# Hymba encoder layer on one core: the weight-sum unit of eight projection pairs is emitted in another quarter

## The chip, the core and the metric

The kernel runs on one core of a Trainium2 chip. The metric is the device time of one execution in microseconds (us), lower is better. The engines are PE (matrix products), DVE (VectorE), ACT (ScalarE), POOL (GpSimd) and SP, whose queue issues most of the transfers (DMAs). Each engine works through its own list of instructions in order; they wait for one another through semaphores.

## The reference

One bidirectional encoder layer over 1024 prompt rows and 256 sample rows of width 2048:

```python
hn = rmsnorm(x, norm_w)
proj = jnp.einsum('btd,dp->btp', hn, w_in)
na_q, na_k, na_v, na_g, ml_qk, ml_v, ml_o, ml_z, ml_gp = jnp.split(proj, cuts, axis=-1)
att = neighbourhood_attention(na_q, na_k, na_v, na_rpb) * silu(na_g)
qk = silu(centred_depthwise_conv(ml_qk, conv_w, conv_b))
h = rmsnorm(bidirectional_mlstm(mq, mk, mv, gates), head_norm_w)
mem = h * sigmoid(ml_o) * silu(ml_z)
y = x + concat(att, mem) @ w_out
```

After it stands a last rmsnorm of y. Everything is float32.

## The kernel before

Every product is made in three passes: each operand is split into a high part, cast by ACT to the matmul's format (fp32r), and a low part, the difference, made by DVE; PE then forms high*high, high*low and low*high (`split_a`, lines 159 to 161, and `mm_c`).

The stage that the change touches is the input projection of the first 768 rows, `pair_a` (line 328). One call computes a *pair*: two blocks of 128 output columns. It uses a 2x2 block scheme with seven products in place of eight, numbered 1 to 7 and run in the order 1, 5, 6, 4, 7, 2, 3. The sum over the input dimension is cut into four *quarters*, r = 0 to 3. In each quarter

- SP loads 128x1024 raw weights into a buffer of the ring `ra`, which has three (line 367, tile `A48r` for pair A48),
- POOL forms the four weight sums of products 5, 6, 7 and 3 (line 372, tile `A48t`; ring of four),
- ACT casts and DVE subtracts for each of the seven products (lines 160 and 161, tile `A48s`; ring of eight),
- PE runs six matmuls for each product, 42 in a quarter and 168 in a pair (line 190, accumulators `A48b`).

In the last quarter `fold` adds the seven accumulators into the two result tiles `A48c` on DVE (line 340), each read freeing a PSUM bank, and `out_scaled` multiplies by the row scales (line 167). Products 1, 5 and 6 use three banks of one tag, so product 6 of a pair can't start before product 5 of the pair ahead has been folded.

What is left of a pair is done by the generator `finish_a`, stepped while the next pair runs. The order of pairs repeats in fours (`order`): a qk pair, whose convolution (lines 270 to 282) is DVE work during the pair behind it; a v pair (n1 from 56 on, such as A68); and two more. A v pair's result is transposed by PE (line 310, tile `A68v`, 12 small instructions), copied by ACT and stored by SP (line 313), all in the pair that follows it.

Into this stage are put 32 *weight-sum units* (`wsum_unit`, line 316), which work ahead for the output projection at the end of the kernel. A unit loads 128x1024 weights into a buffer of the same ring `ra` with a DMA that POOL issues (line 319), adds and subtracts in four POOL instructions of 128x256 (lines 321 to 324), and stores the result to DRAM (line 326). The units are handed to `pair_a` by the loop over the pairs, by position i. Most pairs take one unit, emitted ahead of the load of quarter r = 1; pairs with i % 4 == 1 take two from i = 6 on, at r = 1 and r = 3; v pairs (i % 4 == 3) take none. The build's scheduler then fixes each engine's order from the emitted program, so a unit's instructions can land among those of the pair ahead.

The pairs right behind a v pair, i % 4 == 0, are A8, A12, A16, A20, A40, A44, A48 and A52.

Of the kernel before, what the change touches and what calls it, by code (L numbers as in the profile page):

```python
# [24 lines left out]
NCH = 56  # L25
# [13 lines left out]
def kernel(  # L39
# [27 lines left out]
    def bank(tag, name):  # L67
        return ps.tile([P, 512], F32, tag=tag, name=name, bufs=3 if tag == "pr" else 5)
# [43 lines left out]
    def x_square(g, i):  # L112
        t, q = divmod(i, 2)
        r0 = GOF[g] + t * P
        raw = wa.tile([P, 1024], F32, tag="ra", name=f"xq{g}_{i}", bufs=NRA)
        DM.dma_start(raw, xtok[r0 : r0 + P, q * 1024 : (q + 1) * 1024])
        S.activation(raw, raw, AF.Square, accum_out=ssq[g][:, t, q : q + 1])

    def x_rstd(g):
        n = GSZ[g] // P  # L120
        rc = rcs[g][:, :n]
        V.tensor_reduce(rc, ssq[g][:, :n], axis=mybir.AxisListType.X, op=ALU.add)
        rsqrt_mean(rc, rc, n, float(D))
# [35 lines left out]
    def split_a(hi, lo, src):  # L159
        S.copy(hi, src)  # L160
        V.tensor_tensor(lo, src, f(hi), op=ALU.subtract)

    def out_scaled(o, src, rb, n):
        if n < KT0:
            V.scalar_tensor_tensor(o, src, float(P) ** -0.5, rb, op0=ALU.mult, op1=ALU.mult)
        else:
            V.tensor_tensor(o, src, rb, op=ALU.mult)  # L167
# [14 lines left out]
    def xop(i, kk, b_):  # L182
        if i == 1:
            return xb11[kk][:, b_]
        g_, c = XSLOT[i]
        return xg[g_, kk][:, b_, c]

    def mm_c(o, w, x, first, last):
        for m, (a_, b_) in enumerate(((0, 0), (0, 1), (1, 0))):
            PE.matmul(o, w(a_), x(b_), start=first and m == 0, stop=last and m == 2)  # L190

    def pc(name):
        return wa.tile([P, GA], F32, tag="pc", name=name, bufs=NPC)

    def wsa(name):
        return wa.tile([P, 2, 256], F32R, tag="wsa", name=name, bufs=NWS)
# [89 lines left out]
    def finish_a(n1, Cn):  # L286
        nm = f"A{n1}"
        for j in range(2):
            if n1 >= NCH:
                break  # L290
            if QK0 <= n1 < OT0:
                ct = n1 - QK0 + j
                DM.dma_start(qb[ct], Cn[j][:, GA - 4 :])
                cv = pc(f"{nm}cv{j}")
                yield from conv_taps(cv, Cn[j], ct, GA - 2, 2)
                DM.dma_start(cD[ct][:, : GA - 2], cv[:, : GA - 2])
            else:
                if OT0 <= n1 < ZT0:
                    S.activation(Cn[j], Cn[j], AF.Tanh, scale=0.5)
                elif n1 >= GT0:  # L300
                    th = pc(f"{nm}th{j}")
                    S.activation(th, Cn[j], AF.Tanh, scale=0.5)
                    V.scalar_tensor_tensor(Cn[j], th, 1.0, Cn[j], op0=ALU.add, op1=ALU.mult)
                DM.dma_start(pT[n1 + j][:, 0:GA], Cn[j])
            yield
        if n1 >= NCH:
            for tt in range(GA // P):
                b = bank("a", f"{nm}v{tt}")
                for j in range(2):
                    PE.transpose(b[:, j * P : (j + 1) * P], Cn[j][:, tt * P : (tt + 1) * P], ident)  # L310
                o = wa.tile([P, 256], F32, tag="vo", name=f"{nm}vo{tt}", bufs=2)
                S.copy(o, b[:, :256])
                DM.dma_start(vD[(n1 - NCH) // 2][tt * P : (tt + 1) * P, :], o)
                yield

    def wsum_unit(u):
        raw = wa.tile([P, 1024], F32, tag="ra", name=f"wsum{u}", bufs=NRA)
        t = raw.rearrange("p (s c) -> p s c", s=4)
        G.dma_start(raw, w_os[u])  # L319
        a11, a12, a21, a22 = (t[:, i] for i in range(4))  # L320
        G.tensor_tensor(a22, a21, a22, op=ALU.add)
        G.tensor_tensor(a21, a11, a21, op=ALU.subtract)
        G.tensor_tensor(a11, a22, a11, op=ALU.subtract)
        G.tensor_tensor(a12, a12, a11, op=ALU.subtract)
        cp, c0 = u // 16, u % 16 * 256
        G.dma_start(sD[cp][:, :, c0 : c0 + 256], t)

    def pair_a(n1, bg=iter(()), hook=None, units=()):
        nm = f"A{n1}"
        tags = ("pr", "pr", "pr", "a", "a", "a", "a")  # L330
        order = (1, 5, 6, 4, 7, 2, 3)
        bk = {i: bank(t, f"{nm}b{i}")[:, :HALF] for i, t in zip(order, tags)}
        Cn = [pc(f"{nm}c{j}") for j in range(2)]
        C = [Cn[q // 2][:, (q % 2) * HALF : (q % 2 + 1) * HALF] for q in range(4)]

        def scaled(q):
            out_scaled(C[q], C[q], rbs[0][:, (q % 2) * HALF : (q % 2 + 1) * HALF], n1)

        def plus(q, src, i):
            V.tensor_tensor(C[q], C[src], bk[i], op=ALU.add)  # L340

        def fold(i):
            if i == 1:
                S.copy(C[0], bk[1])
            elif i == 6:
                plus(1, 0, 6)
            elif i == 7:
                plus(2, 1, 7)
                plus(3, 2, 5)
                plus(1, 1, 5)  # L350
                plus(2, 2, 4)
                scaled(3)
                scaled(2)
            elif i == 2:
                plus(0, 0, 2)
                scaled(0)
            elif i == 3:
                plus(1, 1, 3)
                scaled(1)

        for r in range(4):
            if r == 2 and hook is not None:
                hook()
            if r in (1, 3) and r // 2 < len(units):
                wsum_unit(units[r // 2])
            raw = wa.tile([P, 1024], F32, tag="ra", name=f"{nm}r{r}", bufs=NRA)
            DM.dma_start(raw, w_in[n1 // 2, r])
            A = {(j, f_): raw[:, (2 * j + f_) * 256 :][:, :256] for j in range(2) for f_ in range(2)}

            def summed(i, x, y_, op):  # L370
                t = wa.tile([P, 256], F32, tag="wt", name=f"{nm}t{r}{i}", bufs=NWT)
                G.tensor_tensor(t, x, y_, op=op)
                return t

            src = {1: A[0, 0], 4: A[1, 1], 2: A[0, 1]}
            for i in order:
                if i == 5:
                    src[5] = summed(5, A[1, 0], A[1, 1], ALU.add)
                elif i == 6:
                    src[6] = summed(6, src[5], A[0, 0], ALU.subtract)  # L380
                elif i == 7:
                    src[7] = summed(7, A[0, 0], A[1, 0], ALU.subtract)
                elif i == 3:
                    src[3] = summed(3, A[0, 1], src[6], ALU.subtract)
                t = wsa(f"{nm}s{r}{i}")
                split_a(t[:, 0], t[:, 1], src[i])
                for q in range(2):
                    kk = 2 * r + q
                    mm_c(
                        bk[i], lambda a_: t[:, a_, q * P : (q + 1) * P],  # L390
                        lambda b_: xop(i, kk, b_), kk == 0, kk == 7,
                    )
                if r == 3:
                    fold(i)
                elif i in (5, 4, 2):
                    next(bg, None)
        for _ in bg:
            pass
        return finish_a(n1, Cn)
# [48 lines left out]
    order = [4, 6]  # L448
# [11 lines left out]
    bg = iter(())  # L460
    units = list(range(32))
    for i, n1 in enumerate(order):
        n = 0 if n1 >= NCH else 2 if i % 4 == 1 and 5 < i < 30 else 1
        bg = pair_a(n1, bg, second_pools if i == len(order) - 1 else None, units[:n])
        del units[:n]
        if i == 1:
            gates_a()
        k = i - 4
        if 0 <= k < 8:
            x_square(1, k)  # L470
        if k == 8:
            x_rstd(1)
# [1034 lines left out]
```

## Time and profile before

| what | value |
|---|---|
| time, median of 3 runs | 2667.58 us (2665.68 to 2668.62) |
| time of the profiled execution | 2671.81 us |
| span of its trace, first to last instruction | 2670.1 us |
| mean granted PE clock | 0.991 of full |
| busy share DVE / ACT / POOL | 75% / 52% / 31% |

The span is 1.7 us shorter than the profiled execution's own time; that execution is 4.2 us above the median. A row of a timeline gives the start in us, the length of the stretch in us, the engine, the line of the kernel, what is written and read, the count, and in brackets the idle time before it with what ended it. Rows in which several instructions of one kind follow each other are merged.

### The profile page before, as it was taken

To read this page: it belongs to the slowest core of one execution; us is meant where nothing else is said; L and a number is where in the kernel's file an instruction comes from. 1 tells how busy PE (TensorE), PEld (TensorE's weight loads), DVE (VectorE), ACT (ScalarE), POOL (GpSimd) and SP (SyncE) were. 2 spreads that over 40 slices of the span, in tenths; PEclk is the share of its full clock that TensorE was granted. 3 is DMA by queue.
4 is the path that set the end of the run, shared out by engine and by line. 5 is a ranking of instruction groups with operands and counts; after the bars stand their busy time and mean duration, and the time that the engine had idled before them with its cause. 6 is when DMAs were issued, how large, how long until landed. Compare 5 with 4: busy or idle time off the path is not lost.

```text
span 2670.1 us, 43607 instructions
## 1 busy us (share of the span) xinstructions
PE 2602.4 (97%) x14518; PEld 2382.8 (89%) x14518; DVE 1992.5 (75%) x3962; ACT 1389.2 (52%) x3140; POOL 817.3 (31%) x1021
## 2 busy tenths in 40 slices
PE   8999999999999999999999999999999999999997
PEld 8899999999999999998989989989888878877786
DVE  7868778898878788875487587577567675787775
ACT  7534444444444444453566576566566543566654
POOL 0545566656565565500011011010001000125312
PEclk9999999999999999999999999999999999999999
DMA  6524344434343433454556656655555456779875
GB/s 209 177 91 146 119 158 134 143 118 154 104 149 111 135 119 127 137 176 143 172 166 192 197 153 195 187 158 181 177 180 161 155 177 228 223 252 314 284 225 177
DMA packets 245753, 454.20 MB, mean 170 GB/s; under 512 B 30320, under 2 KB 121624, under 8 KB 245528
## 3 DMA queue, kind: packets, MB, share of 16 engines
q1 hardware_dynamic: 232856, 407.38, 48.3%
q0 software_dynamic: 9216, 33.56, 3.9%
q10 hardware_dynamic: 3456, 10.49, 1.0%
q8 instruction: 114, 1.87, 0.3%
q14 instruction: 111, 0.91, 0.1%
HBM read 368.41 MB, written 82.91 MB: 169 GB/s over the span
## 4 chain that ended last, share of the span: by engine, by line
PE 46%; DMA 7%; DVE 3%; ACT 2%; issue 1%; SPq 1%; POOL 0%; ACTq 0%; POOLq 0%; DVEq 0%
PE pc L514 19%; PE pv L596 4%; PE G00p L1286 3%; PE G11p L1286 3%; PE G10p L1286 2%; PE S L1286 2%; PE G01p L1286 1%; PE A54b L190 1%; PE A52b L190 1%; DMA wr<-in_w_in_dram 1%; DMA nap_0vr<-vD 1%; PE nap_0s L638 1%; PE nap_1s L638 1%; DMA wrS<-in_w_o_dram 0%; PE mlp_2in L942 0%
## 5 line engine op out<-in xcount | busy, mean ns | idle before, releaser
L154 DVE TENSOR_TENSOR ws<-wr,ws 128x512 fp32r<-128x512 f32 x224 | 155.1, 697 | 114.8 <-ACT ws L153 113.9
L153 ACT CAST ws<-wr 128x512 fp32r<-128x512 f32 x224 | 137.5, 619 | 157.8 <-PE pc L514 107.8
L1309 POOL TENSOR_TENSOR y<-y,fn 128x512 f32<-128x512 f32 x40 | 62.5, 1578 | 411.0 <-ACT jk L1308 216.1
L104 POOL TENSOR_SCALAR mls_0r<-mls_0r 128x2 f32<-128x2 f32 x4 | 1.1, 278 | 255.9 <-ACT mls_0jk L1110 255.9
L154 DVE TENSOR_TENSOR ws_S<-wrS,ws_S 128x512 fp32r<-128x512 f32 x64 | 54.5, 883 | 13.9 <-ACT ws_S L153 13.9
L154 DVE TENSOR_TENSOR wsv<-wr_v,wsv 128x512 fp32r<-128x512 f32 x64 | 44.4, 697 | 19.1 <-ACT wsv L153 18.6
L153 ACT CAST wsv<-wr_v 128x512 fp32r<-128x512 f32 x64 | 39.2, 616 | 30.8 <-PE pc L514 18.2
L154 DVE TENSOR_TENSOR ws_G10w<-wrG10w,ws_G10w 128x512 fp32r<-128x512 f32 x56 | 44.4, 816 | 13.4 <-ACT ws_G10w L153 13.2
L1286 PE MATMUL S<-ws_S,xsb 128*128 128x512 f32 x192 | 48.2, 406 | 4.0 <-DVE ws_S L154 2.8
L153 ACT CAST ws_G11w<-wrG11w 128x512 fp32r<-128x512 f32 x56 | 34.6, 620 | 33.2 <-PE G11p L1286 17.3
L154 DVE TENSOR_TENSOR ws_G11w<-wrG11w,ws_G11w 128x512 fp32r<-128x512 f32 x56 | 43.0, 793 | 11.1 <-ACT ws_G11w L153 11.1
L154 DVE TENSOR_TENSOR ws_G01w<-wrG01w,ws_G01w 128x512 fp32r<-128x512 f32 x56 | 45.1, 827 | 8.0 <-ACT ws_G01w L153 6.7
L167 DVE TENSOR_TENSOR pco<-pc,rstdb 128x512 f32<-128x512 f32 x48 | 32.9, 687 | 23.3 <-PE pc L514 22.4
L1286 PEld LDWEIGHTS S<-ws_S,xsb 128*128 128x128 f32 x192 | 36.8, 194 | 14.3 <-DVE ws_S L154 4.5
L276 DVE SCALAR_TENSOR_TENSOR pcv<-pco,cw_sb,pcv 128x516 f32<-128x516 f32 x64 | 47.9, 758 | 0.8 <-ACT pcv L270 0.8
L153 ACT CAST ws_S<-wrS 128x512 fp32r<-128x512 f32 x64 | 37.7, 617 | 18.4 <-PE S L1286 10.8
L319 POOL DMA_DIRECT2D wsum<-in_w_os_dram x32 | 18.5, 577 | 92.2 <-DMA xq<-in_xtok_dram 76.9
L153 ACT CAST ws_G10w<-wrG10w 128x512 fp32r<-128x512 f32 x56 | 33.8, 618 | 23.7 <-PE G10p L1286 10.0
L153 ACT CAST ws_G01w<-wrG01w 128x512 fp32r<-128x512 f32 x56 | 34.3, 619 | 22.7 <-PE G01p L1286 12.4
L514 PE MATMUL pc<-x_2h,ws 128*128 128x512 f32 x112 | 44.6, 398 | 0.9 <-ACT ws L153 0.9
L1286 PE MATMUL S<-ws_S,xsv 128*128 128x512 f32 x192 | 45.3, 393 | 0.0
L514 PE MATMUL pc<-x_6h,ws 128*128 128x512 f32 x112 | 44.5, 397 | 0.5 <-ACT ws L153 0.5
(1824 smaller groups left out, 9335.9 us busy)
## 6 DMA issues: line engine op xcount, KB each, us to landing
wr<-in_w_in_dram SPq DMA_DIRECT2D x112, 512.0 KB
wsum<-in_w_os_dram POOLq DMA_DIRECT2D x32, 512.0 KB, 4.1
sD<-wsum POOLq DMA_DIRECT2D x32, 512.0 KB, 3.3
wr_v<-in_w_in_dram SPq DMA_DIRECT2D x32, 512.0 KB
wrS<-in_w_o_dram SPq DMA_DIRECT2D x64, 256.0 KB
xq<-in_xtok_dram SPq DMA_DIRECT2D x20, 512.0 KB
xr<-in_xtok_dram SPq DMA_DIRECT2D x40, 256.0 KB
wrG00w<-sD SPq DMA_DIRECT2D x32, 256.0 KB
```

Of the source, the lines that this page charges most:

```text
L104: E.tensor_scalar(out, ssum, 1.0 / count, EPS, op0=ALU.mult, op1=ALU.add)
L153: S.copy(hi, src)
L154: V.tensor_tensor(lo, src, f(hi), op=ALU.subtract)
L167: V.tensor_tensor(o, src, rb, op=ALU.mult)
L190: PE.matmul(o, w(a_), x(b_), start=first and m == 0, stop=last and m == 2)
L276: V.scalar_tensor_tensor(dst[:, a:n], src[:, a + j - pad : n + j - pad], cw_sb[:, ct, j : j + 1], dst[:, a:n], op0=ALU.mult, op1=ALU.add,)
L319: G.dma_start(raw, w_os[u])
L514: PE.matmul(pb[j], t[:, wi, c : c + P], xs, start=r == 0 and f_ == 0 and q == 0 and wi == 0 and xs is xh, stop=r == 3 and f_ == 1 and q == ...
L596: PE.matmul(outs[tt], xs[:, tt * P : (tt + 1) * P], t[:, wi, q * w : (q + 1) * w], start=first and m == 0 and (gates or tt % 2 == 0), stop ...
L638: PE.matmul(b[:, :nkeys], qs(a_), ks(b_), start=i == 0, stop=i == 2)
L1286: PE.matmul(bk[s_], x_[:, xi, s_ * P : (s_ + 1) * P], t[:, wi, :512], start=first and m == 0, stop=last and m == 2,)
L1309: G.tensor_tensor(yc, yc, fn[nb], op=ALU.mult)
```

## The change

In a pair that follows a v pair the unit is emitted at r = 3 in place of r = 1. `pair_a` now takes a dictionary from quarter to unit; all other pairs keep their units and quarters, and the units keep their order.

```diff
-    def pair_a(n1, bg=iter(()), hook=None, units=()):
+    def pair_a(n1, bg=iter(()), hook=None, units={}):
...
-            if r in (1, 3) and r // 2 < len(units):
-                wsum_unit(units[r // 2])
+            if r in units:
+                wsum_unit(units[r])
...
-        n = 0 if n1 >= NCH else 2 if i % 4 == 1 and 5 < i < 30 else 1
-        bg = pair_a(n1, bg, second_pools if i == len(order) - 1 else None, units[:n])
-        del units[:n]
+        quarters = [(3,), (1, 3) if 5 < i < 30 else (1,), (1,), ()][i % 4]
+        take = {r: units.pop(0) for r in (quarters if i > 1 else (1,))}
+        bg = pair_a(n1, bg, second_pools if i == len(order) - 1 else None, take)
```

On POOL, at the border of v pair A68 and pair A48, the order before was this (`A68t`, `A48t` are the weight sums of line 372; the number behind a name tells one buffer from the next):

```order
 L372 TENSOR_TENSOR A68t_10451<-A68r_10407 128x256
-L319 DMA wsum_10595<-in_w_os_dram 128x1024
 L372 TENSOR_TENSOR A68t_10479<-A68r_10407,A68t_10430 128x256
 L372 TENSOR_TENSOR A48t_10515<-A48r_10504 128x256
-L321 TENSOR_TENSOR wsum_10595<-wsum_10595 128x256
 L372 TENSOR_TENSOR A48t_10532<-A48t_10515,A48r_10504 128x256
-L322 TENSOR_TENSOR wsum_10595<-wsum_10595 128x256
 L372 TENSOR_TENSOR A48t_10558<-A48r_10504 128x256
-L323 TENSOR_TENSOR wsum_10595<-wsum_10595 128x256
 L372 TENSOR_TENSOR A48t_10584<-A48r_10504,A48t_10532 128x256
-L324 TENSOR_TENSOR wsum_10595<-wsum_10595 128x256
```

The unit's load, its four sums and, one row further down, its store leave this place; the pair's own sums of the first quarter now stand there alone.

Further down on POOL, among the sums of A48's second and third quarter, the order of the changed kernel is this:

```order
L372 TENSOR_TENSOR A48t_10649<-A48r_10595 128x256
L319 DMA wsum_10759<-in_w_os_dram 128x1024
L372 TENSOR_TENSOR A48t_10675<-A48r_10595,A48t_10623 128x256
L321 TENSOR_TENSOR wsum_10759<-wsum_10759 128x256
L322 TENSOR_TENSOR wsum_10759<-wsum_10759 128x256
L372 TENSOR_TENSOR A48t_10697<-A48r_10686 128x256
L323 TENSOR_TENSOR wsum_10759<-wsum_10759 128x256
L372 TENSOR_TENSOR A48t_10708<-A48t_10697,A48r_10686 128x256
L324 TENSOR_TENSOR wsum_10759<-wsum_10759 128x256
L372 TENSOR_TENSOR A48t_10728<-A48r_10686 128x256
L326 DMA sD_162<-wsum_10759 512x1x256
```

The load now stands ahead of the last sum of the second quarter, the four sums behind it and among the sums of the third.

On SP the loads of the raw weights move with the ring (`cD` are the stores of the convolved qk pair, `vD` those of the transposed v pair):

```order
 L367 DMA A48r_10504<-in_w_in_dram 128x1024
+L367 DMA A48r_10595<-in_w_in_dram 128x1024
 L296 DMA cD_157<-A36cv_10194 128x766
 L296 DMA cD_158<-A36cv_10317 128x766
-L367 DMA A48r_10602<-in_w_in_dram 128x1024
-L367 DMA A48r_10693<-in_w_in_dram 128x1024
+L367 DMA A48r_10686<-in_w_in_dram 128x1024
 L367 DMA A48r_10766<-in_w_in_dram 128x1024
-L367 DMA A50r_10860<-in_w_in_dram 128x1024
 L313 DMA vD_125<-A68vo_10529 128x256
 L313 DMA vD_125<-A68vo_10555 128x256
 L313 DMA vD_125<-A68vo_10581 128x256
```

The load of A48's second quarter goes ahead of the stores `cD`; the first load of the next pair, A50, goes behind the third store `vD`. DVE's instructions are the same in the same order throughout; those of PE and ACT are too, but for the pairs A8 and A12, where some transposes and one squaring of rows of x (line 117) stand a few places later.

## Prediction

> **What bounds the kernel now.** I read the busy shares first, then the groups of instructions by line for PE, then the timelines of PE, DVE and POOL around one place.
>
> ```profile
> PE 2602.4 (97%) x14518; PEld 2382.8 (89%) x14518; DVE 1992.5 (75%) x3962; ACT 1389.2 (52%) x3140; POOL 817.3 (31%) x1021
> ```
>
> PE is busy nearly all the time, so time is won only where PE waits or runs slowly. The groups show where that is in the stage of the pairs (columns: count, then busy us and mean ns of one, then idle time ahead of them with its releaser).
>
> ```profile
> L190 PE MATMUL A12b<-xg,A12s 128*128 128x384 f32 x144 | 29.6, 360 | 2.9 <-DVE A58c L340 2.9
> L190 PE MATMUL A40b<-xg,A40s 128*128 128x384 f32 x144 | 28.8, 352 | 2.6 <-DVE A64c L340 2.6
> L190 PE MATMUL A48b<-xg,A48s 128*128 128x384 f32 x144 | 28.6, 351 | 3.0 <-DVE A68c L340 3.0
> L190 PE MATMUL A8b<-xg,A8s 128*128 128x384 f32 x144 | 27.3, 340 | 3.0 <-DVE A56c L340 2.9
> ...
> L190 PE MATMUL A56b<-xg,A56s 128*128 128x384 f32 x144 | 25.6, 334 | 0.0
> ```
>
> A pair costs 25.6 us in this group with no idle time (A56). The eight pairs behind a v pair are the exception: each waits 2.6 to 3.1 us for line 340, the fold of the v pair on DVE, and its matmuls are longer by 1.7 (A8) to 4.0 us (A12); the four rows not shown lie at A48's numbers within 0.2 us. These eight are also the pairs whose unit moves. I take A48 as the pattern.
>
> ```profile
> 190.05 1.20 PE L190 MATMUL A56b<-xb,A56s 128*128 128x384 f32 x6
> 219.18 1.20 PE L190 MATMUL A8b<-xb,A8s 128*128 128x384 f32 x6
> 957.27 1.20 PE L190 MATMUL A48b<-xb,A48s 128*128 128x384 f32 x6
> 958.49 1.28 PE L190 MATMUL A48b<-xg,A48s 128*128 128x384 f32 x6
> 962.73 1.30 PE L190 MATMUL A48b<-xg,A48s 128*128 128x384 f32 x6 [2.95 <-DVE A68c L340]
> 965.74 0.42 PE L310 MATMUL A68v<-ident,A68c 128*128 128x128 f32 x1
> 977.76 1.23 PE L190 MATMUL A48b<-xb,A48s 128*128 128x384 f32 x6
> 992.85 1.20 PE L190 MATMUL A50b<-xb,A50s 128*128 128x384 f32 x6
> ```
>
> A pair without loss takes 219.18 - 190.05 = 29.13 us, 0.173 us for each of 168 matmuls. A48 takes 992.85 - 957.27 = 35.58, so it loses 6.45. The parts: product 5 starts 0.18 late (958.49 against 957.27 + 6 x 0.173 = 958.31); product 6 starts 3.20 late (962.73 against 958.49 + 1.04 = 959.53); then the clock.
>
> ```profile
> 223.00:227.00 4.00, 2.33 (x12) 2.04 (x12) 4.00 (x9) 0.41 (x1) 0.91 (x2) 1.00 0.68 227
> 961.00:965.00 4.00, 2.27 (x10) 2.30 (x11) 4.00 (x10) 0.41 (x1) 0.91 (x2) 0.86 0.67 211
> 965.00:969.00 4.00, 4.00 (x19) 3.74 (x19) 4.00 (x8) 0.43 (x2) 1.94 (x3) 0.71 0.27 105
> ```
>
> In these stretches of 4 us (busy time of PE, PEld, DVE, ACT, POOL, then the granted clock) A48's clock falls to 0.86 and 0.71 behind its wait: (0.14 + 0.29) x 4 = 1.72 us lost. A8's stays at 1.00. What is left of A48's loss, 6.45 - 0.18 - 3.20 - 1.72 = 1.35, goes to the 12 transposes of line 310 and their seams. And DVE is busy for the whole 4.00 us of all three: here DVE, not PE, sets the pace.
>
> **What makes DVE late, and what the change removes.** DVE's timeline at that place, then POOL's:
>
> ```profile
> 953.41 0.96 DVE L161 TENSOR_TENSOR A68s<-A68r,A68s 128x256 fp32r<-128x256 f32 x1
> ...
> 956.04 1.84 DVE L161 TENSOR_TENSOR A48s<-A48t,A48s 128x256 fp32r<-128x256 f32 x2
> 957.80 0.54 DVE L340 TENSOR_TENSOR A68c<-A68c,A68b 128x384 f32<-128x384 f32 x1
> 958.27 0.86 DVE L161 TENSOR_TENSOR A48s<-A48r,A48s 128x256 fp32r<-128x256 f32 x1
> 959.05 1.51 DVE L161 TENSOR_TENSOR A48s<-A48t,A48s 128x256 fp32r<-128x256 f32 x1
> 960.49 0.54 DVE L340 TENSOR_TENSOR A68c<-A68c,A68b 128x384 f32<-128x384 f32 x1
> 960.96 0.70 DVE L161 TENSOR_TENSOR A48s<-A48r,A48s 128x256 fp32r<-128x256 f32 x1
> 961.58 1.94 DVE L340 TENSOR_TENSOR A68c<-A68c,A68b 128x384 f32<-128x384 f32 x4
> ...
> 963.90 0.41 DVE L161 TENSOR_TENSOR A48s<-A48t,A48s 128x256 fp32r<-128x256 f32 x1
> ...
> 964.70 0.91 DVE L167 TENSOR_TENSOR A68c<-A68c,rstdb 128x384 f32<-128x384 f32 x1
> ```
>
> ```profile
> 950.96 1.37 POOL L321 TENSOR_TENSOR wsum<-wsum 128x256 f32<-128x256 f32 x1
> 952.28 0.92 POOL L372 TENSOR_TENSOR A48t<-A48t,A48r 128x256 f32<-128x256 f32 x1
> 953.17 0.92 POOL L322 TENSOR_TENSOR wsum<-wsum 128x256 f32<-128x256 f32 x1
> ...
> 954.92 0.92 POOL L323 TENSOR_TENSOR wsum<-wsum 128x256 f32<-128x256 f32 x1
> ...
> 956.68 0.92 POOL L324 TENSOR_TENSOR wsum<-wsum 128x256 f32<-128x256 f32 x1
> 958.12 0.73 POOL L372 TENSOR_TENSOR A48t<-A48r 128x256 f32<-128x256 f32 x1 [0.52 <-DMA A48r<-in_w_in_dram]
> 958.79 0.72 POOL L326 DMA_DIRECT2D sD<-wsum  x1
> ```
>
> The same subtraction takes 0.41 us while POOL is idle (963.90) and 0.96 while a POOL sum runs (953.41). So one POOL sum that meets a subtraction holds DVE up by 0.96 - 0.41 = 0.55 us. Folds, which read PSUM, are always 0.54, whatever POOL does. The chain up to PE is: the fourth fold-step, second of the four at 961.58, ends at 961.58 + 0.47 + 0.54 = 962.59, and product 6 starts at 962.73.
>
> - The **four sums of the unit** (950.96 to 957.60) each stretch one DVE instruction ahead of the first fold: 4 x 0.55 = 2.2 us go.
> - The unit's **store** is issued at 958.79 for 0.72 us, with a sum right behind; the subtraction beside them takes 1.51. With the sum alone it should take 0.96 at most: 0.55 goes, and up to 1.10 if that sum falls beside a fold.
> - The pair's own three sums of the second quarter come earlier, since the **raw load** takes the ring buffer that the unit had and POOL's wait of 0.52 for it goes. They can stretch 958.27 and 960.96 as now, or meet folds; worth 0 to 0.3.
>
> DVE's shift is thus 2.2 us (the sums alone) to 3.6 (2.2 + 1.1 + 0.3). I take 3.0, between 2.75 with the store's smaller price and 3.6.
>
> **What is late next.** With 3.0 the fold lets product 6 start at 962.73 - 3.0 = 959.73. PE would be ready at 957.27 + 12 x 0.173 = 959.35, as product 5's 0.18 goes as well: a wait of 0.38 is left. Behind product 6 stand twelve matmuls in all (2.08 us, to 961.81), then the first transpose, which needs line 167's result: that ended at 964.70 + 0.91 = 965.61 and now at 962.61, so PE waits another 0.8 to 0.9. In A8, the pair with the full clock, this second wait shows already:
>
> ```profile
> PE A56v L310 <- DVE A56c L167: 0.6, 1, 0.6
> ```
>
> So A48 keeps 0.38 + 0.86 of waits and 1.35 of transposes, 2.6 in place of 6.45. It gains 3.86, if the clock stays up, which the shorter gaps should bring: A8 had no drop with one gap of 2.94 and another of 0.6.
>
> **The Trainium skill on the clock**, in "TensorE: Matmul & The Clock Gate", section "What's actually happening", says that PE falls to half its clock after an idle window of about 3.4 us, and that the window runs freely. The trace has the drop behind shorter gaps (2.95), and once, at A8, none behind a gap as long, so the gap's place in the window seems to count. Read strictly, the rule has no drop behind any gap here, before or after; the pair's gain would then be 3.86 - 1.72 = 2.1 and the sum 18 us. The trace's rows decide for the 1.72.
>
> **What is added.** The unit's load, four sums and store now stand at A48's second and third quarter. The four sums and the store can stretch DVE by the same 2.75 us there. But from 970 on DVE has idle time of its own, as it waits for ACT. The first unit sum stands behind the fourth sum of the second quarter, and can't start before its load lands:
>
> ```profile
> 970.73 0.42 DVE L161 TENSOR_TENSOR A48s<-A48t,A48s 128x256 fp32r<-128x256 f32 x1 [0.33 <-ACT A48s L160]
> ...
> DMA to landing us min/median/max: 3.3/3.9/8.1
> ```
>
> The load's buffer is that of the first quarter, free after the subtraction at 960.96 (958.7 in the new time), so the data are there at about 958.7 + 0.6 + 3.9 = 963.2. By then the scaling that the first transposes need is done (962.61). I put this part at 0, covered by DVE's idle time; without it it costs up to 2.75 a pair (a rival below).
>
> SP's load of the next pair's first quarter now goes behind the third store `vD`:
>
> ```profile
> 970.48 0.33 SPq L367 DMA_DIRECT2D A50r<-in_w_in_dram  x1
> ...
> 975.47 0.32 SPq L313 DMA_DIRECT2D vD<-A68vo  x1
> ...
> 985.52 0.41 ACT L160 CAST A50s<-A50r 128x256 fp32r<-128x256 f32 x1 [0.58 <-PE A48b L190]
> ```
>
> So it moves from 970.48 to about 975.8, all of it some 4 us earlier in the new time, and ACT's first use at 985.52 moves as well: 9.7 us are left for a transfer of about 4 us (3.9 above for the same size). No cost.
>
> **The sum.** Six pairs like A48 gain 3.86: 23.2. A8 had no slow clock and follows DVE's chain through both waits: 3.0. A12's matmuls were 1.0 us longer than A48's, by a longer slow stretch: 3.86 + 1.0 = 4.9. Together 31 us. The profiled execution's own 2671.81 would become 2641; from the median of 2667.58 I predict **2636 us**. With a shift of 2.2 a pair of A48's kind gains 0.8 less (eight times: 25 us, 2643); with 3.6 it gains 0.6 more (36 us, 2632); with transposes dearer or cheaper by 0.3 a pair, 2629 to 2645.
>
> **Rivals.**
>
> 1. *The clock still drops.* Two gaps of 0.4 and 0.9, or of 1.2 and 0.9 with the small shift, may fall into one window. For it: seven of eight pairs dropped. Against it: A8 did not with 2.94 and 0.6. Then six pairs lose the 1.72 and A12 2.7 of the gain: 31 - 13 = 18 us, **2650 us**.
> 2. *The hold-up is only moved.* If the unit's sums reach DVE ahead of the scaling of line 167, they hold up the transposes instead: the second wait becomes 0.86 + 2.75 = 3.6 and eats the 3.2 that product 6 gains, with the slow clock behind it. That gives **2663 to 2668 us**. For it: DVE has no idle time until 970. Against it: the load can't land before 962.6 unless it takes under 3.3 us. The Trainium skill, "SBUF — State Buffer", section "SBUF: two separate sides", speaks for this rival: it calls the port that DVE and GpSimd share an exclusive lock, held for a whole instruction, so a moved sum costs DVE as much in its new place. The 0.55 of these rows agrees.
> 3. *Slower: POOL stands behind the load.* In the new order the unit's first sum is ahead of all sums of the third quarter, so a late load stops these, then ACT, DVE and PE. The sums are needed about 1.5 us before PE's third quarter, which began at 977.76, now near 974. The load lands at 963.2, with 9 us to spare; it would have to take 14 us more before the gain is used up, and the longest of 32 took 8.1. Beyond that point each us costs 8: with 15 us more, **2675 us**.
>
> That the change does nothing is excluded by the order shown above.
>
> **How the numbers follow.** The forecast has 70% (2629 to 2645), rival 1 16%, rival 2 10%, rival 3 4%. From 2629 to 2652 lie the forecast and most of rival 1. A measurement of this kernel tells about 0.2% (5.3 us) from no change: faster than 2662.3 are the forecast, rival 1 and a part of rival 2, 0.90; the rest of rival 2 is no change, 0.06; slower 0.04.
>
> **What the changed profile would show.** If right: no POOL instruction of line 321 to 324 in the last 7 us of a v pair; the wait for line 340 in the eight pairs under 1.3 us; a wait for line 167 of 0.5 to 1.2 at the first transpose; clock 1.00 in these stretches; pair A48 at 31 to 33 us. If DVE's 0.96 stays although the unit is gone, the price per sum is wrong. If the wait at line 167 is near 3.6, rival 2 holds; if POOL waits for the unit's load and ACT for POOL in the third quarter, rival 3.

## The result and the profile after

| | before | changed |
|---|---|---|
| median, us | 2666.63 (4 runs, 2663.17 to 2668.62) | 2647.47 (4 runs, 2642.46 to 2650.84) |
| profiled execution, us | 2671.81 | 2650.84 |
| its span, us | 2670.1 | 2649.1 |

The ratio is 0.9928, with a 95% interval of 0.9906 to 0.9949: 19.2 us faster by the medians, 21.0 by the two profiled executions. The forecast was 2636, so about a third of the expected 31 us did not come. The median lies above the forecast's own range of 2629 to 2645.

The page of the changed kernel, busy times of the engines:

```profile
PE 2592.8 (98%) x14518; PEld 2372.1 (90%) x14518; DVE 1989.0 (75%) x3962; ACT 1386.2 (52%) x3140; POOL 819.0 (31%) x1021
```

PE is 9.6 us less busy (slower matmuls that are gone), so the rest of the 21, 11.4, is idle time that is gone. The groups by line for PE, changed kernel, with the idle time ahead at the end of a row:

```profile
L190 PE MATMUL A40b<-xg,A40s 128*128 128x384 f32 x144 | 27.5, 340 | 0.1
...
L190 PE MATMUL A12b<-xg,A12s 128*128 128x384 f32 x144 | 27.5, 340 | 0.4 <-DVE A58c L340 0.4
...
L190 PE MATMUL A48b<-xg,A48s 128*128 128x384 f32 x144 | 27.5, 340 | 0.1
...
L190 PE MATMUL A14b<-xg,A14s 128*128 128x384 f32 x144 | 27.4, 350 | 2.3 <-ACT A14s L160 2.3
```

The waits of 2.6 to 3.1 us for line 340 have gone from all eight pairs but for 0.4 in A12, and their groups stand at 27.5 us, A8's too (27.3 before, with no slow clock). A14, which was free, now waits 2.3 us for ACT. A48's place in PE's timeline of the changed kernel:

```profile
941.56 1.20 PE L190 MATMUL A48b<-xb,A48s 128*128 128x384 f32 x6
942.60 2.62 PE L190 MATMUL A48b<-xg,A48s 128*128 128x384 f32 x12
945.06 0.51 PE L190 MATMUL A48b<-xb,A48s 128*128 128x384 f32 x2
...
946.87 0.33 PE L310 MATMUL A68v<-ident,A68c 128*128 128x128 f32 x1 [0.60 <-DVE A68c L167]
...
973.67 1.20 PE L190 MATMUL A50b<-xb,A50s 128*128 128x384 f32 x6
```

A48 takes 973.67 - 941.56 = 32.11 us in place of 35.58. The small wait ahead of product 6 has no row of its own: the twelve matmuls of products 5 and 6 take 945.06 - 942.60 = 2.46, where 12 x 0.173 = 2.08 were needed, so 0.38 is inside that row. DVE at the same place, changed kernel:

```profile
938.71 1.29 DVE L161 TENSOR_TENSOR A48s<-A48t,A48s 128x256 fp32r<-128x256 f32 x2
939.92 0.54 DVE L340 TENSOR_TENSOR A68c<-A68c,A68b 128x384 f32<-128x384 f32 x1
940.38 0.49 DVE L161 TENSOR_TENSOR A48s<-A48r,A48s 128x256 fp32r<-128x256 f32 x1
940.80 0.95 DVE L161 TENSOR_TENSOR A48s<-A48t,A48s 128x256 fp32r<-128x256 f32 x1
...
942.78 1.94 DVE L340 TENSOR_TENSOR A68c<-A68c,A68b 128x384 f32<-128x384 f32 x4
...
945.90 0.91 DVE L167 TENSOR_TENSOR A68c<-A68c,rstdb 128x384 f32<-128x384 f32 x1
```

The four folds stand 942.78 - 941.56 = 1.22 us behind the pair's start on PE; before it was 961.58 - 957.27 = 4.31. DVE has moved by 3.09. The first fold moved by 2.17: it starts 1.64 ahead of the pair (939.92), before it started 0.53 behind it (957.80). The scaling that the first transpose needs ends at 945.90 + 0.91 = 946.81. The unit's first sum starts just behind that, when its load has landed; POOL, changed kernel:

```profile
947.07 1.15 POOL L321 TENSOR_TENSOR wsum<-wsum 128x256 f32<-128x256 f32 x1 [0.67 <-DMA wsum<-in_w_os_dram]
```

The clock, in stretches of 4 us of the changed kernel (columns as before; the first is A48's, the second A14's):

```profile
941.00:945.00 4.00, 3.87 (x23) 3.58 (x22) 4.00 (x8) 1.40 (x4) 1.78 (x3) 1.00 0.12 29
...
396.00:400.00 4.00, 4.00 (x14) 3.84 (x15) 4.00 (x10) 2.99 (x10) 2.23 (x4) 0.59 0.60 139
```

From 200 us to the end of the stage this stretch at A14 is the only one below 0.95; before there were twelve, in seven of the eight pairs.

The pairs' lengths, from the first matmul of a pair to that of the next (29.1 is a pair without loss):

| pair | before | changed | changed, another execution |
|---|---|---|---|
| A8 / A12 | 35.0 / 36.7 | 32.1 / 32.5 | 32.1 / 32.2 |
| A16 / A20 | 35.6 / 35.6 | 31.9 / 33.9 | 31.9 / 35.7 |
| A40 / A44 | 35.3 / 35.6 | 32.1 / 32.0 | 31.9 / 32.2 |
| A48 / A52 | 35.6 / 35.6 | 32.1 / 32.0 | 31.9 / 31.9 |
| over 29.13, all eight | 51.9 | 25.5 | 26.8 |
| A14 | 29.1 | 33.4 | 32.3 |

The eight pairs gain 26.4 us; A14 loses 4.3 of it, and 1.1 are lost elsewhere. That is less than executions differ: from the last pair on alone, the two of the changed kernel are 4.3 us apart. Two pairs stand out, A20 and A14. What they wait for, by PE's waits of the changed kernel (total us, times, longest):

```profile
PE A14b L190 <- ACT A14s L160: 2.3, 1, 2.3
PE A62v L310 <- ACT A62vo L312: 1.8, 1, 1.8
PE A68v L310 <- DVE A68c L167: 0.6, 1, 0.6
```

The third row stands for eight alike, one in each pair behind a v pair. The first two are new, and lead to ACT and from there to SP's queue. SP around A48, first before, then changed (a row spans merged issues, so its length is mostly waiting):

```profile
954.43 8.11 SPq L367 DMA_DIRECT2D A48r<-in_w_in_dram  x3
970.48 0.33 SPq L367 DMA_DIRECT2D A50r<-in_w_in_dram  x1
970.89 11.72 SPq L313 DMA_DIRECT2D vD<-A68vo  x5
```

```profile
937.64 15.80 SPq L367 DMA_DIRECT2D A48r<-in_w_in_dram  x2
953.53 4.91 SPq L313 DMA_DIRECT2D vD<-A68vo  x3
```

The unit now stands in the ring ahead of the fourth quarter's raw load, so that load needs the buffer of the second quarter and waits at the head of SP's queue for it: 15.1 us at the longest, where no such wait for DVE was over 7.8 in these pairs before, nor over 9.0 in any. (The longest wait for a unit's store is alike in both, 10.8 and 10.9.) The stores `vD` queue behind it. ACT has two buffers for its copies (line 312), so the third copy waits until the first store has landed, and behind that copy stand casts. In A20 this reaches PE; ACT, then PE, changed kernel:

```profile
599.44 0.37 ACT L312 COPY A62vo<-A62v 128x256 f32<-128x256 f32 x1 [5.22 <-DMA vD<-A62vo]
```

```profile
599.86 0.44 PE L310 MATMUL A62v<-ident,A62c 128*128 128x128 f32 x2 [1.80 <-ACT A62vo L312]
```

In A14 it is the squaring of rows of x, whose load uses the same ring. ACT, then SP's own waits there, changed kernel:

```profile
394.39 1.06 ACT L117 ACTIVATE xq<-xq 128x1024 f32<-128x1024 f32 x1 [7.01 <-DMA xq<-in_xtok_dram]
```

```profile
SPq L116 <- DMA sD<-wsum: 10.7, 1, 10.7
```

The load of `xq` stands 10.7 us at SP's head, until a unit's store `sD` has freed its buffer (5.2 before), and ACT, with the casts of A14 behind the squaring, stands 7.0 (4.3 before, which did not reach PE).

### The profile page after: what moved, and what is told of

Same layout as the page of the kernel before. It is cut to its first block, busy times and chain, and to the rows that moved or that the text cites. A ratio compares the mean times of both kernels' runs of the same rounds, so it can differ in the third digit from the quotient of the medians.

```text
span 2649.1 us, 43618 instructions
## 1 busy us (share of the span) xinstructions
PE 2592.8 (98%) x14518; PEld 2372.1 (90%) x14518; DVE 1989.0 (75%) x3962; ACT 1386.2 (52%) x3140; POOL 819.0 (31%) x1021
## 4 chain that ended last, share of the span: by engine, by line
PE 47%; DMA 5%; DVE 3%; ACT 2%; issue 1%; POOL 1%; SPq 0%; ACTq 0%; POOLq 0%; DVEq 0%
PE pc L514 20%; PE pv L596 4%; PE G00p L1286 3%; PE G11p L1286 3%; PE S L1286 2%; PE G10p L1286 2%; PE G01p L1286 1%; PE A54b L190 1%; PE A52b L190 1%; DMA wr<-in_w_in_dram 1%; PE nap_1s L638 1%; PE nap_0s L638 1%; DMA nap_0vr<-vD 1%; DMA wrG10w<-sD 0%; PE mlp_2in L942 0%
## 5 line engine op out<-in xcount | busy, mean ns | idle before, releaser
L153 ACT CAST ws_G10w<-wrG10w 128x512 fp32r<-128x512 f32 x56 | 33.9, 619 | 24.7 <-PE G10p L1286 11.0
L153 ACT CAST ws_G00w<-wrG00w 128x512 fp32r<-128x512 f32 x48 | 29.4, 620 | 31.0 <-PE G00p L1286 17.3
L154 DVE TENSOR_TENSOR ws_G00w<-wrG00w,ws_G00w 128x512 fp32r<-128x512 f32 x48 | 36.3, 775 | 12.4 <-ACT ws_G00w L153 11.7
```

## The experiments

Times of before are those taken beside each group of runs: 2667.72 for `again`, `nosums`, `quarter2` and `behind_load`, 2667.36 for `vd_act`, `xq_away`, `elsewhere` and `behind_all`, 2668.72 for `two_sums`, `behind_xq` and `behind_load2`. "Eight pairs" is their sum over 29.13 each, as in the table. Where only one execution was timed there is no interval.

**`again`: the changed kernel once more.** No edit; this asks whether the waits at A14 and A20 are chance.

> The changed kernel once more, for its trace. Theory (queue): the load of a pair's fourth quarter now waits for a buffer at the head of SP's queue and holds the stores vD behind it, so ACT's third copy waits 3 to 4 us for a vD store in all eight pairs again; whether this reaches PE depends on when a store lands, so the waits of PE at A14 (2.3) and A20 (1.8) may come and go. Rival: the two waits belong to their places (the squaring of x rows at A12, nothing else), then A14's 2.3 returns and A20's does not. Time 2642 to 2651 by both.

2649.39 us. PE waits 2.8 in A14 for ACT and 2.2 in A20 for the copies of A62v. Both came back in the same places, so they are hardly chance; with the 2.2 in A20 came a stretch at a clock of 0.69, while the 2.8 in A14 left the clock at 1.00. It does not show which part of the order makes them.

**`nosums`: the kernel before, without the four sums in the eight units.** Their part of the first output is left out; the loads and stores stay where they were.

```diff
-        G.tensor_tensor(a22, a21, a22, op=ALU.add)
-        G.tensor_tensor(a21, a11, a21, op=ALU.subtract)
-        G.tensor_tensor(a11, a22, a11, op=ALU.subtract)
-        G.tensor_tensor(a12, a12, a11, op=ALU.subtract)
+        if sums:      # False for the unit of a pair behind a v pair
+            ... the same four
```

> The kernel before, with the four sums left out in the eight units behind a v pair; their load, buffer and store stay where they were. Theory (POOL's sums hold up DVE): the four sums' 2.2 us go, so the wait for line 340 falls from 2.9 to about 0.8, the clock stays at 1.00 in these pairs, they take about 33 us in place of 35.6, and the time falls by 16 to 22 us to 2645 to 2651. Rival (the gain of the change came from the ring buffer that the raw load of the second quarter gets earlier): nothing moves, 2667, wait 2.9, clock drop in seven pairs.

2637.75 us, 30 under before; eight pairs 21.8, no slow clock in them. DVE, PE and POOL of this kernel:

```profile
934.63 0.54 DVE L341 TENSOR_TENSOR A68c<-A68c,A68b 128x384 f32<-128x384 f32 x1
...
936.23 0.94 DVE L161 TENSOR_TENSOR A48s<-A48r,A48s 128x256 fp32r<-128x256 f32 x1
937.09 1.93 DVE L341 TENSOR_TENSOR A68c<-A68c,A68b 128x384 f32<-128x384 f32 x4
```

```profile
935.67 1.20 PE L190 MATMUL A48b<-xb,A48s 128*128 128x384 f32 x6
...
938.24 1.28 PE L190 MATMUL A48b<-xg,A48s 128*128 128x384 f32 x6 [0.33 <-DVE A68c L341]
```

```profile
929.81 0.73 POOL L327 DMA_DIRECT2D sD<-wsum  x1 [0.50 <-DMA wsum<-in_w_os_dram]
```

The folds stand 937.09 - 935.67 = 1.42 behind the pair's start, a shift of 2.9, with the unit's load, store and ring buffer in their old order. The second quarter's raw load goes out 3.3 us ahead of the pair's start, hardly earlier than before (2.8), where the changed kernel has 10.6. So the old waits come from the unit's POOL work beside DVE, not from the ring. The store keeps its place in the order but not in time: it is issued 5.9 us ahead of the pair's start, where it was issued 1.5 behind it (958.79), so its part is not separated from that of the sums here. The gain was expected at 16 to 22 and is 30, more than the whole change brings.

**`two_sums`: as `nosums`, but only the last two of the four left out.**

```diff
+        G.tensor_tensor(a22, a21, a22, op=ALU.add)
+        G.tensor_tensor(a21, a11, a21, op=ALU.subtract)
         if sums:
-            G.tensor_tensor(a22, a21, a22, op=ALU.add)
-            G.tensor_tensor(a21, a11, a21, op=ALU.subtract)
             G.tensor_tensor(a11, a22, a11, op=ALU.subtract)
             G.tensor_tensor(a12, a12, a11, op=ALU.subtract)
```

> The kernel before, with the last two of the four sums (lines 323 and 324 of the kernel before) left out in the eight units that stand behind v pairs; their part of out[0] is not the reference's. Sum theory (each sum that meets a subtraction holds DVE up by 0.55 us, and PE's wait for line 340 is what is left of that): with two of four gone DVE's shift is 1.1 to 1.5 us, the waits for line 340 fall from 2.6 to 3.1 to 1.2 to 2.0 us; a pair gains its wait and whatever of the slow clock goes with it: 2650 to 2660 us. Rival (what holds DVE up is the unit as a whole: its load and store, or the first sum alone, and not each sum): the waits stay over 2.4 (2664 to 2669), or all but vanish as with four sums gone (2637 to 2641).

2645.84 us, eight pairs 27.8: it misses the expected range and both of the rival's, and lies between them. PE's start of A48, DVE and POOL of this kernel:

```profile
940.18 1.20 PE L190 MATMUL A48b<-xb,A48s 128*128 128x384 f32 x6
```

```profile
940.31 0.41 DVE L161 TENSOR_TENSOR A48s<-A48r,A48s 128x256 fp32r<-128x256 f32 x1
940.65 0.41 DVE L161 TENSOR_TENSOR A48s<-A48t,A48s 128x256 fp32r<-128x256 f32 x1
940.98 0.54 DVE L341 TENSOR_TENSOR A68c<-A68c,A68b 128x384 f32<-128x384 f32 x1
941.45 0.41 DVE L161 TENSOR_TENSOR A48s<-A48r,A48s 128x256 fp32r<-128x256 f32 x1
941.78 1.93 DVE L341 TENSOR_TENSOR A68c<-A68c,A68b 128x384 f32<-128x384 f32 x4
```

```profile
937.80 0.72 POOL L327 DMA_DIRECT2D sD<-wsum  x1
...
941.48 0.98 POOL L373 TENSOR_TENSOR A48t<-A48r 128x256 f32<-128x256 f32 x1 [2.18 <-DMA A48r<-in_w_in_dram]
```

The shift is 4.31 - (941.78 - 940.18) = 2.7, where two sums were to give 1.1 and the store 0.4 more at best. The three subtractions ahead of the folds take 0.41 each; before they took 0.86, 1.51 and 0.70. So 1.84 of the 2.7 come from here: POOL is through with the unit earlier, the store too is issued 2.4 us ahead of the pair's start, and POOL then stands 2.18 for the next raw load, so nothing runs beside DVE in these two us. The remaining 0.86 is left for the two sums, priced at 1.1. How many meetings go does not follow from the sums taken out: the store and the pair's own sums move too. The waits for line 340 are gone in all eight pairs; instead PE waits 0.5 to 1.0 us in each for an ACT cast, in A48 one that waits for POOL's sum behind that late load. The eight pairs keep 6 us more than in `nosums`.

**`quarter2`: the units at r = 2.**

```diff
-        quarters = [(3,), (1, 3) if 5 < i < 30 else (1,), (1,), ()][i % 4]
+        quarters = [(2,), (1, 3) if 5 < i < 30 else (1,), (1,), ()][i % 4]
```

> The changed kernel with the eight units emitted at quarter r = 2 in place of 3. The second quarter's raw load is early as in the change; the unit's load goes out some 8 us earlier than in the change, so its sums meet the folds and scalings of the v pair. Theory (POOL's sums hold up DVE): the transposes wait 1.5 to 2.5 us for line 167 in place of 0.8, the eight pairs take 33 to 34.5 us in place of 32, time about 2655. Rival (ring): the pairs stay at 32.0, time 2642 to 2651.

2647.45 us, the same as the changed kernel; eight pairs 27.5. POOL, PE's longest new wait and SP:

```profile
940.79 0.73 POOL L321 TENSOR_TENSOR wsum<-wsum 128x256 f32<-128x256 f32 x1 [1.33 <-DMA wsum<-in_w_os_dram]
```

```profile
PE A58v L310 <- ACT A58vo L312: 2.1, 1, 2.1
```

```profile
940.95 10.97 SPq L367 DMA_DIRECT2D A48r<-in_w_in_dram  x2
```

The expected wait of 1.5 to 2.5 for line 167 did not come (0.6 to 0.7): the sums begin only when their load has landed, 940.79, and fall among the folds, which they do not stretch (the four folds take 1.93). PE waits for ACT's copies instead, 1.0 to 2.1 us in four pairs and 0.3 to 0.5 in three. In A44 and A48 the copies stand behind `vD` and SP's raw load, as in the changed kernel (ACT waits 4.7 and 4.6); in A8 and A12 (the 2.1 above) they stand behind the squaring of x, whose load is late (ACT waits 4.3 and 5.5). As far as one execution shows, the fourth quarter is not needed; leaving the v pair's end is.

**`behind_load`: the units still in the fourth quarter, but emitted behind its raw load.** The ring then serves that load ahead of the unit.

```diff
             DM.dma_start(raw, w_in[n1 // 2, r])
+            if r + 4 in units:
+                wsum_unit(units[r + 4])
...
-        quarters = [(3,), (1, 3) if 5 < i < 30 else (1,), (1,), ()][i % 4]
+        quarters = [(7,), (1, 3) if 5 < i < 30 else (1,), (1,), ()][i % 4]
```

> The changed kernel with the eight units still in r = 3, but emitted behind that quarter's raw load in place of ahead of it. The raw load then takes the first quarter's buffer, some 8 us before it does in the change, and SP's stores vD no longer stand behind a waiting load. Theory (queue): ACT's wait for a vD store falls from 3.2 to 5.2 us to about 1.3 as before the change, PE's waits at A14 and A20 go, and the time is 2640 to 2644, some 4 to 6 us under the change. Rival (the waits are those of slow landings or of the squaring of x rows): they stay, time as the change, 2645 to 2650.

2640.51 us, ratio 0.9899 (0.9882 to 0.9915). Eight pairs 22.2, A14 29.1. SP:

```profile
929.89 5.62 SPq L367 DMA_DIRECT2D A48r<-in_w_in_dram  x2
942.73 4.45 SPq L313 DMA_DIRECT2D vD<-A68vo  x3
```

Both raw loads leave within 5.62 us, the stores no longer stand behind one, ACT has no wait for `vD` at all, and the waits in A14 and A20 are gone. The gain is 27.2 us by the medians, where the changed kernel has 19.2, though the two intervals still overlap (0.9915 and 0.9906 are their near ends). In the traces the eight pairs fall by 25.5 - 22.2 = 3.3 us and A14 by 4.3, 7.6 in all.

**`vd_act`: the changed kernel with the stores `vD` issued by ACT.**

```diff
-                DM.dma_start(vD[(n1 - NCH) // 2][tt * P : (tt + 1) * P, :], o)
+                S.dma_start(vD[(n1 - NCH) // 2][tt * P : (tt + 1) * P, :], o)
```

> The changed kernel, with the stores vD of the v pairs issued by ACT in place of SP, so that they no longer stand behind a raw load that waits for its ring buffer. Queue theory (SP's order is what the change costs): ACT's waits for vD (3.4 to 5.2 us in the changed kernel) fall under 2, A20's wait for ACT of 1.8 goes, xq's load behind them is on time, so A14's wait of 2.3 goes or falls under 1; A20 near 32.0 and A14 near 29.5 us; time 2640 to 2645. Rival (the ring itself, with three buffers, is what makes the fourth quarter late, whoever stores): the waits at A14 and A20 stay, 2647 to 2652. ACT's own time for three issues a v pair could cost something on PE: then other waits for ACT appear, 2650 or more.

2643.22 us, ratio 0.9904 (0.9887 to 0.9920). ACT's waits for `vD` are gone and A20 is at 31.9: that half holds. The other half fails in its reason: A14's wait falls under 1 as expected, but not because `xq` is on time. ACT's and PE's waits:

```profile
ACT xq L117 <- DMA xq<-in_xtok_dram: 33.9, 8, 7.2
```

```profile
PE A58v L310 <- ACT A58vo L312: 1.3, 1, 1.3
...
PE A14b L190 <- ACT A14s L160: 0.8, 1, 0.8
```

`xq` is as late as ever, so it was not late because of the stores; why A14's wait is shorter is not shown. A14 keeps 30.4 us, and A8 and A12 grow to 33.0 and 33.5, where copies stand behind the squaring on ACT.

**`xq_away`: the changed kernel, the squarings out of the pairs behind v pairs.**

```diff
+    XQ = (5, 6, 7, 9, 10, 11, 13, 14)
...
-        k = i - 4
-        if 0 <= k < 8:
-            x_square(1, k)
-        if k == 8:
+        if i in XQ:
+            x_square(1, XQ.index(i))
+        if i == 15:
             x_rstd(1)
```

> The changed kernel, with the eight row squarings of x (line 117) moved from positions 4 to 11 of the loop to positions 5, 6, 7, 9, 10, 11, 13 and 14, so that none stands in a pair behind a v pair. Queue theory: PE's wait of 2.3 in A14 goes (A14 near 29.3 us), A20's wait for the copies of A62v stays at 1.5 to 2.2, ACT still waits 3.4 to 5.5 for vD: time 2643 to 2646 (4.3 us less than the changed kernel at the most). Rival (A14's wait comes from ACT's own load there, not from xq's late transfer): the wait stays or moves to the pair that takes the squaring, 2647 to 2651.

2642.53 us, ratio 0.9900 (0.9883 to 0.9916), just under the expected 2643 to 2646. A14 has no wait and takes 29.1 us; A20 keeps 33.7. PE's and ACT's waits:

```profile
PE A62v L310 <- ACT A62vo L312: 1.4, 1, 1.4
```

```profile
ACT A62vo L312 <- DMA vD<-A62vo: 4.8, 1, 4.8
```

With `vd_act` this separates the two: A20 waits for the stores behind SP's raw load, A14 for the load of `xq`, which needs a buffer of the same ring of three.

**`elsewhere`: the eight units moved into qk pairs.**

```diff
-        quarters = [(3,), (1, 3) if 5 < i < 30 else (1,), (1,), ()][i % 4]
+        quarters = [(), (1, 3) if 5 < i < 30 else (1,), (1, 3), ()][i % 4]
```

> The eight units leave the pairs behind v pairs altogether and are emitted at r = 3 of the pairs with i % 4 == 2 (the qk pairs are emitted at i % 4 == 2 or beside), units in another order of positions. If the unit's place in its pair were what is left of the loss: the eight pairs go to 31.9 us, no wait for vD over 2 us, as in the run with the load ahead (2640.5), and no new waits elsewhere: 2638 to 2643. Rival (the sums' cost of 0.55 each on DVE is only carried to a place where DVE is late as well, the end of the v pair's or qk pair's quarter): waits for line 340 or for DVE over 1 us appear in other pairs, 2645 to 2665.

2643.29 us, ratio 0.9907 (0.9890 to 0.9923), at the upper end of what was expected. The pairs behind v pairs take 31.9 to 32.6, with line-340 waits of 0.8 in A12 and A16; the v pair A60 takes 31.0 and A28 30.6. So there are small new waits (the longest 1.1, for ACT in A28), none for DVE of the rival's size.

**`behind_all`: all 32 units behind the raw load of their quarter.**

```diff
-            if r in units:
-                wsum_unit(units[r])
             raw = wa.tile([P, 1024], F32, tag="ra", name=f"{nm}r{r}", bufs=NRA)
             DM.dma_start(raw, w_in[n1 // 2, r])
+            if r in units:
+                wsum_unit(units[r])
```

> The changed kernel with every unit of all pairs emitted behind the raw load of its quarter in place of ahead of it (the run behind_load did so for the eight alone: 2640.5 us). Queue theory: the eight pairs as there (31.8 to 32.1 us), A14 and A20 free of waits; the other 24 units lose little, as no wait stands there now: 2637 to 2642. Rival (a unit behind its quarter's load is late for its buffer and holds POOL's sums of the next quarter): POOL waits for wsum of over 2 us and PE waits for ACT or DVE appear in pairs with two units: 2645 to 2660.

2642.47 us, ratio 0.9900 (0.9885 to 0.9914). Eight pairs 22.1, but A10 takes 31.2, with a wait for ACT of 1.7. The time is just above the expected 2637 to 2642; nothing is won beyond the eight.

**`behind_xq` and `behind_load2`: both repairs at once, and `behind_load` again beside it.** The edits are those of `behind_load` and `xq_away` together.

> Both repairs of the changed kernel at once: the eight units emitted behind the raw load of the fourth quarter (2640.5 us alone) and the row squarings of x out of the pairs behind v pairs (2642.5 us alone). If both take away the same cost, SP's order around the v pairs, they do not add: A14, A20 free of waits, eight pairs at 31.8 to 32.1, 2638 to 2641. If they took away different costs (7 and 5 us), 2634 to 2637.

> The kernel with the eight units behind the raw load of the fourth quarter once more, beside the kernel with both repairs on the same chip: 2638 to 2643, no wait of PE for ACT in A14 or A20. If the waits there were chance, one returns and a pair of 33 us or more with it.

2638.76 us, ratio 0.9889 (0.9874 to 0.9903), and 2642.22 us, ratio 0.9899 (0.9883 to 0.9915). Eight pairs 21.8 and 22.4; no wait of PE for ACT in A14 or A20 in either. The intervals overlap, so the two are not told apart, and it is not shown that the repairs add; together they do not reach 2634 to 2637. Both beat the kernel before and, by the medians, the changed one by 5 to 9 us; of the two only the interval of `behind_xq` lies clear of the changed kernel's (0.9906 to 0.9949).

## Why the prediction was right in direction and too large

**The number.** 2647.47 is above the range given to the forecast and 2.5 below rival 1's 2650. That it comes near rival 1 is chance: the clock, which that rival needs, did not drop where it says, and what was lost went into new waits and into transposes that cost more than forecast.

**The place and the mechanism: right.** DVE shifted by 3.09, against 3.0 taken; `nosums` shows that the unit's sums cause the waits, with the store that moves with them. In the changed kernel the shift also has the parts that were forecast: 2.17 at the first fold, ahead of which the unit's four sums stood (2.2 taken), and 0.92 between it and the four folds, for the store and the pair's own sums. That this split fitted so well is in part luck: with other sums taken out it comes out otherwise. At the first fold `nosums` moved DVE by only 0.53 + 935.67 - 934.63 = 1.57, four sums gone as well. In `two_sums` the stretch behind the first fold gave 1.84, of which the store explains 1.10 at most, so the term "own sums, 0 to 0.3" was too narrow: what counts is every POOL instruction that meets a subtraction in the few us ahead of the folds, and which ones do depends on when POOL gets its next load.

**What is late next: right.** Predicted were a wait of 0.38 at product 6 and 0.86 at the first transpose, 1.24 in all. In A48 the first transpose comes 946.87 - 941.56 = 5.31 behind the start, with 24 matmuls (4.16) ahead of it: 1.15.

**The clock: right that it stays up in the eight pairs, its value too high.** Of A48's 6.45 of loss, 965.74 - 957.27 - 4.16 = 4.31 lay ahead of the first transpose, and 2.14 behind it. After, it is 1.15 and 32.11 - 29.13 - 1.15 = 1.83. A gain of 0.31 behind the transpose is all that is seen there, where 0.79 was to come: 1.72 for the clock and 1.35 for the transposes were a split of one remainder, and the transposes' share was larger: 1.83. A part can be read from the prediction's own rows. At the full clock the twelve matmuls from 962.73 would have ended at 964.81, and the transposes had to wait for line 167 until 965.61. So the wait that the prediction has behind the change, 0.86, was there before too, and the slow clock ahead of 965 (0.14 x 4 = 0.56) lay within it and cost nothing. Counting both the whole 1.72 and no such wait before made the transposes look cheap. So A48 gained 3.47 in place of 3.86, and the five pairs of its kind without a new wait 3.5 on average: 1.7 us of the sum.

**What is added: this term was mis-sized.** It stood at 0. For the sums and the store that holds, if narrowly: the first sum started at 947.07, when its load had landed, 0.26 behind the end of the scaling at 946.81 (0.6 was forecast). The wait for line 167 stayed at 0.6, and `behind_load` keeps the sums in that quarter without loss. The prediction checked SP's late load of the next pair and found 9.7 us to spare; what it did not follow is the load of the same pair's fourth quarter, which now needs the second quarter's buffer and holds the stores behind it, and the squarings that use the same ring. That cost A14 4.3 us and A20 2.0 (33.9 against 31.9), and in `again` 3.2 and 3.8, there with the slow clock in A20. `xq_away` takes A14's away, `vd_act` A20's, and `behind_load` both. With the gain of the eight pairs 4.6 below the sum (1.7, 0.7 for A8 and A12, 2.2 at A20), A14's 4.3 and 1.1 elsewhere, the account of the two profiled executions closes: 31 - 10 = 21.

**The rivals.** From 200 us to the end of the stage the clock dropped once, in A14, behind one of the new waits, not in any of the eight pairs (in `again` once, in A20, behind a new wait too): rival 1 falls. The wait for line 167 was 0.6, not 3.6: rival 2 falls. The moved sums do stretch DVE's subtractions in their new place (0.95 at 947.54 and 0.96 at 949.43, where 0.41 is the time without), but behind the scaling for which the transposes wait. POOL does stand for late loads, but in no pair does that reach PE by the path of rival 3; its root, the late raw load, did act by another path, through SP's queue to ACT.

**Left open.** The four timed runs of the changed kernel spread from 2642 to 2651; the profiled one of them and `again` lie near the top (2650.84 and 2649.39), and whether the faster ones are free of the waits in A14 and A20 was not seen. Why transposes and seams cost 1.83 a pair was not tried; no kernel here has the eight pairs under 21.8.

## What to carry to other kernels

When work is moved to another place of a ring of buffers, follow each load that now gets another buffer, and everything that stands behind that load on its queue, stores too: an engine may be reached two steps on. A helper engine's sums are worth moving away from the moment at which DVE is last in the chain, but count the meetings in the trace, since the helper's other work moves with them. Emitting the moved work behind the load of its quarter in place of ahead of it took away both new waits here and gave 27 us by the medians in place of 19 (26.5 when repeated).

## What the runs showed of the hardware that was not expected

The clock fell behind shorter gaps than before: behind 2.35 us in A14 (clock 0.59 in that stretch) and behind 2.16 in A20 of `again`. PE there, then the clock in two stretches of 4 us:

```profile
601.54 0.69 PE L310 MATMUL A62v<-ident,A62c 128*128 128x128 f32 x2 [2.16 <-ACT A62vo L312]
```

```profile
600.00:604.00 4.00, 2.46 (x9) 2.47 (x10) 1.97 (x4) 1.87 (x6) 2.63 (x5) 0.69 0.38 68
604.00:608.00 4.00, 4.00 (x23) 3.96 (x22) 1.61 (x3) 1.57 (x4) 1.33 (x3) 0.88 0.69 265
```

So (0.31 + 0.12) x 4 = 1.72 us were lost, exactly A48's sum before. In stretches of 0.5 us the clock reads 0.51 from 601.5, 0.50 from 602.0 to 604.5, and 1.00 again from 605.0: half clock for about 3.4 us. The length of the gap alone does not decide. Gaps of 2.94 (A8 before), 2.76 (A14 of `again`), 2.05 (A12 of `quarter2`) and 1.80 (A20 of the changed kernel) left the clock up. What decides was not tested.

The Trainium skill, "TensorE: Matmul & The Clock Gate", section "What's actually happening", gives an idle window of about 3.4 us as the condition. These rows show 3.4 us as the length of the drop, but not as the least gap.
